# Moving the split weight buffers to other offsets, modulo 512, from the activations in a hybrid decoder layer

## The chip, the cores and the metric

The kernel runs on one core of a Trainium2 chip. TensorE (PE) multiplies, VectorE (DVE) and ScalarE (ACT) work elementwise, GpSimd (POOL) does little here, and SyncE (SP) issues all DMAs. SBUF is the on-chip memory of 128 partitions; an address in it is counted in bytes within a partition. The metric is the device time of one execution in microseconds (us), lower is better. A kernel's time is the median of several runs.

## The reference

One layer on a sequence of 256 tokens of width 2048, in float32: a modulation from a vector c, four token mixers behind one combined input projection, an output projection, a gated FFN with a causal convolution, and a last norm.

```python
mod = (silu(c) @ w_mod + b_mod).reshape(B, 6, D)
sh1, sc1, g1, sh2, sc2, g2 = [mod[:, i, None, :] for i in range(6)]
h = rmsnorm(x, norm_mix) * (1.0 + sc1) + sh1
proj = h @ w_in                                   # 2048 x 5660
y = concat(gla(proj), gated_deltanet(proj), pool(proj), forgetting_attention(proj))
x = x + g1 * (y @ w_out)                          # 2048 x 2048
h = rmsnorm(x, norm_ffn) * (1.0 + sc2) + sh2
gate = causal_dwconv(h @ w_gate, conv_w) + conv_b # 2048 x 5632
x = x + g2 * ((silu(gate) * (h @ w_up)) @ w_down) # 5632 x 2048
return rmsnorm(x, norm_final)
```

## The kernel before

**Three products for one.** Matrices are multiplied in the type fp32r. To keep the accuracy of float32, each operand is split in a high part (the value cast to fp32r) and a low part (what the cast left out), and three products are summed: high by high, high by low, low by high. Activations are split once and kept: `bigA` holds, for each of 16 slices k of the width 2048, the high part of 256 tokens and then the low part; `AH` and `AL` hold the FFN's inner activations. Weights are split as they come. `load` (lines 152 to 156) brings 512 KB into one of five buffers `wr` by a DMA on SP; `load_split` (158 to 163) has ACT cast it into `wh` (line 115) and DVE subtract into `wl` (line 100). There are three buffers `wh` and three `wl`, each 4096 bytes a partition, used in turn.

**The stages and their matmuls**, all recorded on line 97 (`mm`). A matmul has a stationary operand (loaded first, by its own instruction, LDWEIGHTS, 128 columns) and a moving one, which streams.

- Input projection (`gdn`, `pair`): wh or wl stationary, bigA moving, 256 columns; for two of the token-major outputs bigA is stationary and the weights move. Much other work is woven in, above all matrix-vector products of the modulation on DVE (`accumulate`, line 103).
- The mixers, with some input projection between them.
- Output projection (`project`): bigA stationary, wh or wl moving, 512 columns, in the last two chunks 256.
- Gate and up (`proj`): wh or wl stationary, bigA moving. For each k four matmuls of wh with high and low part of bigA side by side, 512 columns, then four of wl with the high part, 256 columns.
- Down projection: AH or AL stationary, wh or wl moving, 512 columns, in the last two chunks 256.

**Where things lie.** Pools take space in SBUF in the order in which they are opened: `keep` first (constants, `bigA`, `bigC`, `ga`, and `x1s` as the last tile), then `wp` (five wr, three wh, three wl, four wm), then the pools of the stages. In the built program bigA starts at 352 modulo 512, and wr, wh, wl, AH and AL all at 416. Every stationary slice (128 columns of 4 bytes) and every step from one k to the next is a multiple of 512 bytes, so the distance of a stationary from a moving operand, modulo 512, is the same for all matmuls of a stage: stationary less moving, called the offset below, is 64 where weights are stationary and bigA moves, 448 where bigA is stationary and weights move, 0 in the down projection.

**What sets the order.** A scheduler orders the instructions of each engine from the program by its own estimate of times, with the waits that follow from the buffers.

Of the kernel before, what the change touches and what calls it, by code (L numbers as in the profile page):

```python
# [8 lines left out]
F32 = mybir.dt.float32  # L9
F32R = mybir.dt.float32r  # L10
# [6 lines left out]
P = 128  # L17
D = 2048
KT = D // P
T = 256  # L20
NT = T // P
# [25 lines left out]
NG = len(GROUPS)  # L47

TAKE = (16, 12, 11)

ORDER = "gpfd"

# [21 lines left out]
def trunk_kernel(ctx: ExitStack, tc: tile.TileContext, x, c, w_mod, b_mod, norm_mix, norm_ffn, w_in,  # L74
# [3 lines left out]
    nc = tc.nc  # L78
# [11 lines left out]
    keep = ctx.enter_context(tc.tile_pool(name="keep", bufs=1))  # L90
    wp = ctx.enter_context(tc.tile_pool(name="wp", bufs=3))

    def kt_(shape, name, dt=F32):
        return keep.tile(shape, dt, name=name, tag=name)
# [19 lines left out]
    def split(hi, lo, src):  # L114
        S_.copy(hi, src)  # L115
        tt(lo, src, hi.bitcast(F32), ALU.subtract)
# [4 lines left out]

    ident = kt_([P, P], "ident")
    nc.sync.dma_start(ident, cst[:, K_ID:K_ID + P])
    crow = kt_([KT, P], "crow")
    nc.sync.dma_start(crow, c[0].rearrange("(k p) -> k p", p=P))
    ones = kt_([P, P], "ones")
    V.memset(ones, 1.0)

# [24 lines left out]
    def load(view, k0, nk, c0, n):  # L153
        wr = wp.tile([P, 1024], F32, name="wr", tag="wr", bufs=5).rearrange("p (k n) -> p k n", n=n)
        nc.sync.dma_start(wr[:, 0:nk], view[:, k0:k0 + nk, c0:c0 + n])  # L155
        return wr

    def load_split(view, k0, nk, c0, n):
        wr = load(view, k0, nk, c0, n)
        wh = wp.tile([P, 1024], F32R, name="wh", tag="wh", bufs=3).rearrange("p (k n) -> p k n", n=n)  # L160
        wl = wp.tile([P, 1024], F32R, name="wl", tag="wl", bufs=3).rearrange("p (k n) -> p k n", n=n)
        split(wh[:, 0:nk], wl[:, 0:nk], wr[:, 0:nk])
        return wh, wl

# [63 lines left out]
    with ExitStack() as ph:  # L228
# [59 lines left out]
        with ExitStack() as st:  # L288
            sp = st.enter_context(tc.tile_pool(name="sp", bufs=1, reuse_waits="tile"))
            acp = st.enter_context(tc.tile_pool(name="acp", bufs=1, space=PSUM, reuse_waits="tile"))  # L290
            xt = sp.tile([P, NT, D], F32, name="xt")
            r1 = sp.tile([P, P], F32, name="r1")
            r2 = sp.tile([54, P], F32, name="r2")
            r3 = sp.tile([2 * NF, P], F32, name="r3")
# [115 lines left out]
            def gdn(g):  # L410
                k0, nk = GROUPS[g]
                for k2 in range(k0, k0 + nk, 2):
                    for c3 in range(3):
                        wh, wl = load_split(wi_v, k2, 2, C_QKV + 512 * c3, 512)
                        for kk in range(2):
                            k = k2 + kk
                            for f in range(4):
                                ft = c3 * 4 + f
                                o = acc[ft // 2][:, ft % 2]
                                fs = slice(f * P, f * P + P)  # L420
                                mm(o, wh[:, kk, fs], HL[:, k, 0:T], start=False, stop=False)
                                mm(o, wh[:, kk, fs], HL[:, k, T:], start=False, stop=False)
                                mm(o, wl[:, kk, fs], HL[:, k, 0:T], start=False, stop=k == KT - 1)
                        yield
# [13 lines left out]
            def pair(p, g0, g1):  # L438
                c0, tok, dst, scale = pairs[p]
                k0, k1 = GROUPS[g0][0], sum(GROUPS[g1 - 1])  # L440
                a = ext().rearrange("p (f t) -> p f t", t=T)
                for ka in range(k0, k1, 4):
                    kb = min(ka + 4, k1)
                    wh, wl = load_split(wi_v, ka, kb - ka, c0, 256)
                    for f in range(2):
                        for k in range(ka, kb):
                            fs = slice(f * P, f * P + P)
                            first, last = f == 0 and k == k0, k == k1 - 1
                            if tok:
                                xh, xl = HL[:, k, fs], HL[:, k, T + f * P:T + f * P + P]  # L450
                                three = ((xh, wh[:, k - ka]), (xh, wl[:, k - ka]), (xl, wh[:, k - ka]))
                            else:
                                xh, xl = HL[:, k, 0:T], HL[:, k, T:]
                                three = ((wh[:, k - ka, fs], xh), (wh[:, k - ka, fs], xl), (wl[:, k - ka, fs], xh))
                            for i, (l, r_) in enumerate(three):
                                mm(a[:, f], l, r_, start=first and i == 0, stop=last and i == 2)
                    yield
                with tc.high_priority():
                    add(dst, a, g0 == 0, scale)
# [10 lines left out]
            def extras(g):  # L470
                ps = range(len(pairs) - TAKE[g], len(pairs)) if g < NG - 1 else range(len(pairs))
                for p in ps:
                    yield from pair(p, done[p], g + 1)
                    done[p] = g + 1
# [472 lines left out]
        chunks = ((0, 512), (512, 512), (1024, 512), (1536, 256), (1792, 256))  # L947
        Y2 = bigA()

        def project(n, a):  # L950
            c0, w = chunks[n]
            nk = 1024 // w
            for j in range(KT // nk):
                ks = order[nk * j:nk * j + nk]
                if n == 0:
                    for k in ks:
                        split(Y2[:, k, 0:T], Y2[:, k, T:], pr[:, k + 4])
                wh, wl = load_split(wo_v, ks[0], nk, c0, w)
                steps = [(kk, k, t) for kk, k in enumerate(ks) for t in range(NT)]
                if n == len(chunks) - 1 and ks[-1] == order[-1]:  # L960

                    steps.sort(key=lambda s: s[2])
                for kk, k, t in steps:
                    st, sp_ = j + kk == 0, nk * j + kk == KT - 1
                    xh, xl = Y2[:, k, t * P:t * P + P], Y2[:, k, T + t * P:T + t * P + P]
                    mm(a[t], xh, wh[:, kk], start=st, stop=False)
                    mm(a[t], xh, wl[:, kk], start=False, stop=False)
                    mm(a[t], xl, wh[:, kk], start=False, stop=sp_)
# [5 lines left out]
        x1 = bigC().rearrange("p (t d) -> p t d", t=NT)  # L974
        for t in range(NT):
            nc.sync.dma_start(x1[:, t], x_v[:, t])
        x1s = kt_([P, NT, len(chunks)], "x1s")
        with tc.tile_pool(name="op", bufs=2, reuse_waits="tile") as op:
            for n, (c0, w) in enumerate(chunks):
                ns, gs = slice(c0, c0 + w), slice(c0 % 1024, c0 % 1024 + w)  # L980
# [11 lines left out]
    with ExitStack() as ph:  # L992
# [51 lines left out]
        with tc.tile_pool(name="gp", bufs=2, reuse_waits="tile") as gp:  # L1044
            for n in range(NF // 4):
                gt = proj(gp, wg_v, 512 * n)
                ut = proj(gp, wu_v, 512 * n)
                for i in range(4):
                    f = 4 * n + i
# [12 lines left out]
        with tc.tile_pool(name="op2", bufs=1, reuse_waits="tile") as op:  # L1062
            chunks = ((0, 512), (512, 512), (1024, 512), (1536, 256), (1792, 256))
            fs = op.tile([P, NT, len(chunks)], F32, name="fs")
            f1 = op.tile([P, 4], F32, name="f1")
            for n, (c0, w) in enumerate(chunks):
# [5 lines left out]
                for g in range(NF // nk):  # L1072
                    wh, wl = load_split(wd_v, nk * g, nk, c0, w)
                    for kk in range(nk):
                        k = nk * g + kk
# [55 lines left out]
```

## Time and profile before

| | us |
|---|---|
| median of 3 runs | 1305.72 |
| lowest and highest | 1299.94, 1308.62 |
| the profiled execution | 1303.01 |
| its span, first to last instruction | 1301.2 |
| busy: PE / DVE / ACT | 1248.5 / 891.0 / 636.7 |

The granted clock of TensorE is 0.985 of full speed over the span; the reductions lie at the start and the end. Busy times of PE are sums of overlapping matmuls merged into stretches. A timeline row gives the start of a run of equal instructions, its length, engine, line, operation, output and inputs, shapes, and how many they are. As matmuls overlap in the pipeline, the length of a row is not their pace; the distance from one row's start to the next one's is.

### The profile page before, as it was taken

The numbers are of one execution on the slowest core, as the hardware profiler recorded it, in microseconds if no ns is written. First come the engines' busy times: TensorE is split into PE (matmuls) and PEld (weight loads), VectorE is DVE, ScalarE is ACT, GpSimd is POOL, SyncE is SP. The second block draws the span as 40 slices with busy tenths as digits, with TensorE's granted clock in tenths as the row PEclk, the third lists the DMA queues.
The fourth block names the chain that finished last, engine by engine and source line by source line (L and its number), as shares of the span: only waits on it lengthen the run. The fifth ranks groups of instructions, "written<-read, shape, count | busy, mean of one in ns | idle before, by whom it ended". The sixth has DMA issues, their size and how long they took to land.

```text
span 1301.2 us, 20372 instructions
## 1 busy us (share of the span) xinstructions
PE 1248.5 (96%) x7927; PEld 1091.0 (84%) x7927; DVE 891.0 (68%) x1201; ACT 636.7 (49%) x1000; POOL 22.7 (2%) x31
## 2 busy tenths in 40 slices
PE   2799999999999999999999999999999999999996
PEld 1799999898876788888888888888888888888896
DVE  7689797989763397676656656665656597964543
ACT  3455344774354454564545555554555454443432
POOL 0200000010000100000000000000000000000000
PEclk9799999999999999999999999999999999999998
DMA  9999998796566988556576666666665699875652
GB/s 321 277 367 378 337 341 290 259 339 212 164 236 240 318 317 276 156 165 192 163 214 190 186 187 193 190 172 206 187 187 163 219 374 359 323 243 194 192 181 81
DMA packets 174231, 311.94 MB, mean 240 GB/s; under 512 B 16172, under 2 KB 65331, under 8 KB 173495
## 3 DMA queue, kind: packets, MB, share of 16 engines
q1 hardware_dynamic: 174135, 310.65, 72.9%
q8 instruction: 62, 1.02, 0.3%
q14 instruction: 34, 0.28, 0.1%
HBM read 308.51 MB, written 2.10 MB: 239 GB/s over the span
## 4 chain that ended last, share of the span: by engine, by line
PE 92%; DMA 4%; SPq 1%; DVE 1%; ACT 1%; issue 1%; POOLq 0%; ACTq 0%; DVEq 0%
PE fpt L97 57%; PE ext L97 16%; PE wot L97 5%; PE gdt L97 4%; PE acc L97 4%; PE bgt L97 3%; DMA wm<-in_w_mod_dram 3%; PE oxt L97 2%; DMA wr<-in_w_in_dram 1%; DVE ga L103 1%; DMA ct<-in_cst_dram 0%; ACT xT L1011 0%; DVE wl L100 0%; SPq L399 0%; SPq L155 0%
## 5 line engine op out<-in xcount | busy, mean ns | idle before, releaser
L100 DVE TENSOR_TENSOR wl<-wr,wh 128x1024 fp32r<-128x1024 f32 x384 | 469.2, 1223 | 293.6 <-ACT wh L115 292.6
L115 ACT CAST wh<-wr 128x1024 fp32r<-128x1024 f32 x384 | 403.4, 1051 | 494.9 <-PE fpt L97 310.8
L97 PE MATMUL fpt<-bigA,wh 128*128 128x512 f32 x1408 | 399.6, 395 | 2.1 <-DVE bigA L103 2.1
L97 PEld LDWEIGHTS fpt<-bigA,wh 128*128 128x128 f32 x1408 | 239.3, 189 | 32.8 <-issue 2.2
L97 PEld LDWEIGHTS fpt<-bigA,wl 128*128 128x128 f32 x1408 | 222.4, 188 | 34.4 <-DVE wl L100 3.6
L97 PE MATMUL fpt<-bigA,wl 128*128 128x256 f32 x1408 | 240.4, 279 | 0.0
L103 DVE SCALAR_TENSOR_TENSOR ga<-wm,cond,ga 128x1024 f32<-128x1024 f32 x139 | 177.8, 1279 | 9.5 <-DMA wm<-in_w_mod_dram 8.6
L97 PE MATMUL fpt<-wl,AH 128*128 128x512 f32 (+1 forms) x440 | 152.9, 348 | 0.0
L97 PE MATMUL fpt<-wh,AL 128*128 128x512 f32 (+1 forms) x440 | 152.5, 347 | 0.0
L97 PE MATMUL fpt<-wh,AH 128*128 128x512 f32 (+1 forms) x440 | 142.5, 348 | 0.0
L97 PE MATMUL ext<-bigA,wh 128*128 128x256 f32 x768 | 137.0, 280 | 0.0
L97 PEld LDWEIGHTS ext<-bigA,wh 128*128 128x128 f32 x768 | 117.3, 188 | 3.1 <-DVE dS L100 0.8
L97 PE MATMUL ext<-bigA,wl 128*128 128x256 f32 x384 | 107.2, 280 | 1.7 <-DVE wl L100 1.7
L97 PEld LDWEIGHTS fpt<-wh,AH 128*128 128x128 f32 x440 | 83.3, 189 | 10.7 <-issue 0.2
L97 PEld LDWEIGHTS fpt<-wh,AL 128*128 128x128 f32 x440 | 83.3, 189 | 10.5 <-issue 0.2
L97 PEld LDWEIGHTS fpt<-wl,AH 128*128 128x128 f32 x440 | 83.3, 189 | 10.5 <-issue 0.2
L97 PE MATMUL acc<-bigA,wh 128*128 128x256 f32 x384 | 70.3, 289 | 4.7 <-ACT bigA L115 2.9
L97 PEld LDWEIGHTS ext<-bigA,wl 128*128 128x128 f32 x384 | 72.1, 188 | 3.0 <-DVE wl L100 2.1
L97 PE MATMUL ext<-wh,bigA 128*128 128x256 f32 (+1 forms) x320 | 68.0, 304 | 0.0
L97 PEld LDWEIGHTS acc<-bigA,wh 128*128 128x128 f32 x384 | 60.7, 198 | 5.1 <-ACT bigA L115 3.0
L97 PE MATMUL wot<-wh,bigA 128*128 128x512 f32 (+1 forms) x256 | 63.2, 337 | 0.0
L97 PEld LDWEIGHTS ext<-wh,bigA 128*128 128x128 f32 x320 | 51.7, 188 | 5.5 <-ACT wh L115 1.7
(340 smaller groups left out, 1191.9 us busy)
## 6 DMA issues: line engine op xcount, KB each, us to landing
wm<-in_w_mod_dram SPq DMA_DIRECT2D x192, 512.0 KB, 5.8
wr<-in_w_in_dram SPq DMA_DIRECT2D x88, 512.0 KB, 9.7
wr<-in_ffn_w_gate_dram SPq DMA_DIRECT2D x88, 512.0 KB, 3.9
wr<-in_ffn_w_up_dram SPq DMA_DIRECT2D x88, 512.0 KB, 4.4
wr<-in_ffn_w_down_dram SPq DMA_DIRECT2D x88, 512.0 KB, 4.5
wr<-in_w_out_dram SPq DMA_DIRECT2D x32, 512.0 KB, 4.2
xt<-in_x_dram SPq DMA_DIRECT2D x2, 1024.0 KB, 7.2
bigC<-in_x_dram SPq DMA_DIRECT2D x2, 1024.0 KB, 8.6
```

The source lines that it names most:

```text
L97: PE.matmul(o, lhsT=l, rhs=r, start=start, stop=stop, skip_group_check=True)
L100: V.tensor_tensor(out=o, in0=a, in1=b, op=op)
L103: V.scalar_tensor_tensor(out=o, in0=a, scalar=s, in1=b, op0=op0, op1=op1)
L115: S_.copy(hi, src)
```

## The change

Three things are done to the layout; no instruction is added or removed.

- Each of the three pairs wh, wl gets a name and a buffer of its own (wh0, wl0, wh1 and so on), used in turn as before, and wl0 and wl1 are padded by 64 and 224 bytes. So the pairs lie at three different places modulo 512.
- x1s, the last tile ahead of the weight buffers, is padded from 64 bytes to 160.
- crow (512 bytes, the row form of c) moves from `keep` to the pool `sp` of the first stage, which makes room.

In the built program bigA stays at 352 modulo 512, wr lies at 0, the pairs at 0, 64 and 288, AH and AL at 288. The offset as defined above is then, for the three pairs, 160, 224 and 448 with stationary weights; 352, 288 and 64 with stationary bigA; 288, 224 and 0 in the down projection.

```diff
+APART = (96, 64, 224)
...
-    crow = kt_([KT, P], "crow")
-    nc.sync.dma_start(crow, c[0].rearrange("(k p) -> k p", p=P))
...
+    loads = [0]
+
     def load_split(view, k0, nk, c0, n):
         wr = load(view, k0, nk, c0, n)
-        wh = wp.tile([P, 1024], F32R, name="wh", tag="wh", bufs=3).rearrange("p (k n) -> p k n", n=n)
-        wl = wp.tile([P, 1024], F32R, name="wl", tag="wl", bufs=3).rearrange("p (k n) -> p k n", n=n)
+        i = loads[0] % 3
+        loads[0] += 1
+        wh = wp.tile([P, 1024], F32R, name=f"wh{i}", tag=f"wh{i}", bufs=1)
+        wl = wp.tile([P, 1024], F32R, name=f"wl{i}", tag=f"wl{i}", bufs=1,
+                     padded_shape=[P, 1024 + (APART + (0,))[i + 1] // 4])
+        wh, wl = (w.rearrange("p (k n) -> p k n", n=n) for w in (wh, wl))
         split(wh[:, 0:nk], wl[:, 0:nk], wr[:, 0:nk])
         return wh, wl
...
             xt = sp.tile([P, NT, D], F32, name="xt")
+            crow = sp.tile([KT, P], F32, name="crow")
+            nc.sync.dma_start(crow, c[0].rearrange("(k p) -> k p", p=P))
...
-        x1s = kt_([P, NT, len(chunks)], "x1s")
+        x1s = keep.tile([P, NT, len(chunks)], F32, name="x1s", tag="x1s", padded_shape=[P, NT, (64 + APART[0]) // 8])
```

The order of the instructions is the same on all engines but for one place, early in the first up pass. On ACT, before (wr_5972 and so on are the loads of w_up, in order; lo copies empty the gate pass):

```order
L115 CAST wh_5974<-wr_5972 128x1024
L115 CAST wh_5996<-wr_5994 128x1024
L115 CAST wh_6018<-wr_6016 128x1024
L1040 COPY lo_5934<-fpt_5754 128x256
L1040 COPY lo_5937<-fpt_5755 128x256
L115 CAST wh_6040<-wr_6038 128x1024
```

and after, where the cast of the fourth load stands ahead of the third's:

```order
L117 CAST wh0_5974<-wr_5972 128x1024
L117 CAST wh2_6018<-wr_6016 128x1024
L117 CAST wh1_5996<-wr_5994 128x1024
L1048 COPY lo_5934<-fpt_5754 128x256
L1048 COPY lo_5937<-fpt_5755 128x256
L117 CAST wh0_6040<-wr_6038 128x1024
```

The same pair on DVE, where the low parts are made, before:

```order
L100 TENSOR_TENSOR wl_5975<-wr_5972,wh_5974 128x1024
L100 TENSOR_TENSOR wl_5997<-wr_5994,wh_5996 128x1024
L100 TENSOR_TENSOR wl_6019<-wr_6016,wh_6018 128x1024
L100 TENSOR_TENSOR fpt_5754<-fpt_5754,lo_5934 128x256
L100 TENSOR_TENSOR fpt_5755<-fpt_5755,lo_5937 128x256
```

and after, in the same exchange of places:

```order
L102 TENSOR_TENSOR wl0_5975<-wr_5972,wh0_5974 128x1024
L102 TENSOR_TENSOR wl2_6019<-wr_6016,wh2_6018 128x1024
L102 TENSOR_TENSOR wl1_5997<-wr_5994,wh1_5996 128x1024
L102 TENSOR_TENSOR fpt_5754<-fpt_5754,lo_5934 128x256
L102 TENSOR_TENSOR fpt_5755<-fpt_5755,lo_5937 128x256
```

TensorE takes the third load before the fourth in both.

## Prediction

> **What bounds the kernel now.** I read the page's busy table and chain of waits first, then the busy time by stage, then the groups of instructions by form, and last the timeline of TensorE, row by row, in each stage.
>
> ```profile
> span 1301.2 us, 20372 instructions
> PE 1248.5 (96%) x7927; PEld 1091.0 (84%) x7927; DVE 891.0 (68%) x1201; ACT 636.7 (49%) x1000; POOL 22.7 (2%) x31
> PE 92%; DMA 4%; SPq 1%; DVE 1%; ACT 1%; issue 1%; POOLq 0%; ACTq 0%; DVEq 0%
> 76.00:265.00 189.00, 186.87 (x1590) 181.81 (x1591) 165.64 (x214) 96.31 (x139) 1.46 (x3) 1.00 0.97 326
> 546.00:1041.00 495.00, 492.43 (x2814) 427.38 (x2815) 313.70 (x457) 264.30 (x405) 0.03 (x1) 1.00 0.62 186
> 1041.00:1190.00 149.00, 149.00 (x653) 122.02 (x652) 115.71 (x114) 64.81 (x78) 0.95 (x1) 1.00 0.85 308
> ```
>
> TensorE is busy 96% of the span and carries 92% of the chain. The three stage rows (stretch, length, then busy time of PE, PEld, DVE, ACT and POOL, then granted clock, DMA share, GB/s) are the input projection, gate and up, and the first part of the down projection: TensorE never idles there for more than 1%, the clock is 1.00, and VectorE, the next engine, has room (166 of 189 us at most, 314 of 495 in gate and up). So nothing that ACT, DVE or the DMAs gain or lose by a few ns shows; what counts is the spacing of the matmuls themselves.
>
> Each matmul is preceded by a load of its stationary operand, and the load of the next one runs while the present one streams. The change moves where in SBUF the one lies relative to the other. So the question is whether the spacing of the matmuls depends on that offset. Durations don't tell (they overlap); starts do.
>
> ```profile
> 740.66 1.09 PE L97 MATMUL fpt<-bigA,wh 128*128 128x512 f32 x4
> 741.59 0.62 PE L97 MATMUL fpt<-bigA,wl 128*128 128x256 f32 x4
> 742.05 1.09 PE L97 MATMUL fpt<-bigA,wh 128*128 128x512 f32 x4
> ...
> 645.14 0.40 PE L97 MATMUL fpt<-bigA,wh 128*128 128x512 f32 x1
> ...
> 646.91 0.40 PE L97 MATMUL fpt<-bigA,wh 128*128 128x512 f32 x1
> ```
>
> Gate and up, offset 64 (stationary wh or wl, less moving bigA, modulo 512). One k is four matmuls of 512 columns, 0.93 us or 232.5 ns each, and four of 256, 0.46 us or 115 ns each: 1.39 us a k, 347 ns for a pair of 512 and 256. For a few k the order of the scheduler alternates the two: five pairs between the last two rows take 1.77 us, 354 ns a pair.
>
> ```profile
> 1189.66 0.62 PE L97 MATMUL fpt<-wh,AH 128*128 128x512 f32 x2
> ...
> 1191.93 0.39 PE L97 MATMUL fpt<-wl,AH 128*128 128x512 f32 x1
> 1249.73 0.28 PE L97 MATMUL fpt<-wh,AL 128*128 128x256 f32 x1
> ...
> 1251.41 0.28 PE L97 MATMUL fpt<-wl,AH 128*128 128x256 f32 x1
> ```
>
> Down projection, offset 0 (stationary AH or AL, less moving wh or wl; in the built program both lie at 416 modulo 512). Ten starts in 2.27 us: 227 ns for 512 columns. Fourteen in 1.68 us: 120 ns for 256. Sum of a pair: 347 ns.
>
> ```profile
> 479.65 0.39 PE L97 MATMUL wot<-wh,bigA 128*128 128x512 f32 x1
> ...
> 482.85 0.39 PE L97 MATMUL wot<-wh,bigA 128*128 128x512 f32 x1
> 533.76 0.28 PE L97 MATMUL wot<-wh,bigA 128*128 128x256 f32 x1
> ...
> 536.00 0.28 PE L97 MATMUL wot<-wl,bigA 128*128 128x256 f32 x1
> 239.72 0.28 PE L97 MATMUL ext<-bigA,wh 128*128 128x256 f32 x1
> 240.90 0.28 PE L97 MATMUL ext<-bigA,wl 128*128 128x256 f32 x1
> 249.75 0.28 PE L97 MATMUL ext<-bigA,wh 128*128 128x256 f32 x1
> 251.00 0.28 PE L97 MATMUL ext<-bigA,wh 128*128 128x256 f32 x1
> ```
>
> Output projection, offset 448 (bigA lies 64 before the weights): fourteen in 3.20 us, 228.6 ns for 512; nineteen in 2.24 us, 117.9 ns for 256; a pair 346.5 ns. Input projection, offset 64, 256 columns: ten starts in 1.18 us between the first two rows (118 ns), eleven in 1.25 us between the last two (114 ns): the same instruction at the same offset settles in one of two paces.
>
> So the spacing does depend on something beside the column count: 227 to 232.5 ns for 512 columns, 114 to 120 for 256, at one clock with no wait. But the pair, 512 and 256, costs 346 to 347 ns at all three offsets: what one size gains the other loses.
>
> **The change, part by part.**
>
> *Order.* Nothing moves on PE, POOL and SP. On ACT and DVE one neighbouring pair of splits changes places, early in the first up pass: the fourth load's split now comes ahead of the third's.
>
> ```profile
> 572.83 1.05 ACT L115 CAST wh<-wr 128x1024 fp32r<-128x1024 f32 x1 [1.68 <-PE fpt L97]
> 575.60 1.05 ACT L115 CAST wh<-wr 128x1024 fp32r<-128x1024 f32 x1 [1.73 <-PE fpt L97]
> 578.63 1.09 PE L97 MATMUL fpt<-bigA,wh 128*128 128x512 f32 x4
> 579.56 0.62 PE L97 MATMUL fpt<-bigA,wl 128*128 128x256 f32 x4
> L100 DVE TENSOR_TENSOR wl<-wr,wh 128x1024 fp32r<-128x1024 f32 x384 | 469.2, 1223 | 293.6 <-ACT wh L115 292.6
> ```
>
> The third load's cast ran at 572.83 and the fourth's, which waits for a buffer that TensorE frees, at 575.60. Changed round, the third's cast ends at about 577.7, ahead of its first use at 578.63. Its low part comes after the fourth's on VectorE: 576.65 and two times 1.22 us give 579.1, against a first use at 579.56. Behind the two on ACT stand the copies that empty the gate pass, about 1 us later; their banks are wanted only by the next gate pass, behind the whole of this up pass. Cost 0; the cover is 0.4 us, and if it were gone the cost would be below 1 us, once.
>
> *crow and x1s.* crow's DMA keeps its place as second on SP, so nothing at the start changes. x1s is only spaced wider for one reduction of ten elements. Both 0.
>
> *ACT and DVE on the moved buffers.* Formerly wr, wh and wl were equal modulo 512; now wr is at 0, the pairs at 0, 64 and 288.
>
> ```profile
> L103 DVE SCALAR_TENSOR_TENSOR ga<-wm,cond,ga x139: 1268/1279/1295, 12.7 to 1146.8; 128x1024 f32<-128x1024 f32 x139
> ```
>
> This operation ran with its two inputs 352 bytes apart early on (wm in the pool sp) and 64 apart later, and lies within 1268 and 1295 ns throughout. So I cost the offset there at 0, under the cover of VectorE's free time.
>
> *TensorE.* New offsets: gate, up and most of the input projection 160, 224 and 448, a third of the loads each; output projection 352, 288 and 64; down projection 288, 224 and 0.
>
> ```profile
> L97 PE MATMUL fpt<-bigA,wh 128*128 128x512 f32 x1408 | 399.6, 395 | 2.1 <-DVE bigA L103 2.1
> L97 PE MATMUL fpt<-wl,AH 128*128 128x512 f32 x264 | 103.1, 391 | 0.0
> L97 PE MATMUL fpt<-wl,AH 128*128 128x256 f32 x176 | 49.8, 283 | 0.0
> L97 PEld LDWEIGHTS fpt<-bigA,wh 128*128 128x128 f32 x1408 | 239.3, 189 | 32.8 <-issue 2.2
> L97 PEld LDWEIGHTS ext<-bigA,wsh 128*28 128x28 f32 x32 | 3.3, 104 | 0.3
> ```
>
> Why should the pair be constant? A load of 128 columns takes 85 ns longer than one of 28: 0.85 ns a column of 4 bytes, some 109 ns for its 512 bytes. The moving operand goes by in 0.44 ns a column (227 / 512), 990 bytes in that time. So in every load the stream overtakes it by nearly 512 bytes, one full turn of the distance that the change sets. If they collide at equal addresses modulo 512, the offset decides when, hardly how often. This is my reading; the three equal pair sums are what bears it out.
>
> Sum. Gate and up: 1408 pairs at 347 ns, change 0. Down projection: 3 x 264 = 792 matmuls of 512 and 3 x 176 = 528 of 256, two thirds of them off the offset 0. Nobody has run 224 or 288; between the ends 227 and 232.5, and 114 and 120, I take the mean of the three offsets that ran, 229.4 for 512 (227, 228.6, 232.5) and 117.6 for 256 (120, 117.9, 115): 528 x 2.4 = +1.3 us and 352 x -2.4 = -0.8 us. Output projection and input projection: as likely to gain as to lose, 0. Together +0.5 us on the profiled execution, 1303.01 (1301.2 of it span): 1303.5 us. The median of the runs shown is 1305.72, so the profiled one stands 0.2% under it.
>
> The ends. All at the best pace seen, 227 and 114: gate and up 1408 x (347 - 341) = -8.4 us, down 528 x -6 = -3.2, input projection up to 4 ns on 1590, -6.4: -18, 1285 us. All at the worst, the alternating 354 ns for a pair: 1408 x 7 = +9.9, down 792 x 5.5 = +4.4, input projection +6: +20, 1323 us.
>
> A rule that speaks against the change: the Trainium skill, TensorE: Matmul & The Clock Gate, part 2, says that PE has two independent SBUF read ports, and that loading the next weights takes no read bandwidth from the running matmul. By that rule offsets would cost nothing anywhere and the sum would be 0, 1303 us. The rows agree only in part: they show a matmul of 512 columns at 227 in one place and at 232.5 ns in another with nothing waited for.
>
> **Rivals.**
>
> *Far offsets collide less (faster).* All offsets seen are 0 or 64 either way; 160, 224, 288 and 352 lie far from them. If collisions need nearness, two of the three pairs drop to the best pace, and perhaps the third. For it: 114 ns held for 1.25 us at one offset. Against it: three offsets with one pair sum. Price: up to the whole -18, 1286 us when most of it comes. It decides when a k of gate and up falls under 1.37 us for two of three buffers.
>
> *A worse phase (slower).* The new distances set the long matmuls to collide in every load, as in the alternating order: a pair at 354 ns and the down projection's 512 at 232.5. Price +14 to +20, 1319 us. For it: the matmul of 512 takes 5.5 ns more at 64 than at 0, so losing a good offset in the down projection is real. Against it: the alternating pace came with another order. It decides when a k takes 1.41 us or more.
>
> *It does nothing at all.* The paces are of order, not of address; then every row stays and the time is 1303 us. Its outcome is in the first case.
>
> **How the numbers follow.** Unchanged within 1% (either that the pair sum holds, or that gains and losses by buffer cancel): 0.61. Far offsets: 0.26. Worse phase: 0.13. One per cent, 13 us, is about what a measurement of this kernel can tell from no change; 1286 and 1319 lie just beyond it on each side. The time is that of the likeliest, 1303.5 us; its own range is 1293 to 1314. The range for 8 in 10 takes in both rivals up to their prices: 1285 to 1319.
>
> **What would show it.** In the profile after, gate and up: rows of four wh and four wl alternating with one k in 1.37 to 1.40 us, perhaps with three values that repeat every third load. Down: 512 columns at 227 to 232 ns, 256 at 114 to 120. A k under 1.36 us at any buffer, or 512 columns under 226 ns, would refute the constant pair; a k of 1.41 would be the slower rival. A wait of TensorE for wl near 579 us would be the swapped splits.

## The result, and the profile after

The changed kernel takes 1311.91 us (median of 8 runs, 1310.17 to 1315.08), the one before 1303.95 (8 runs, 1299.94 to 1308.62): ratio 1.0066, 95% interval 1.0050 to 1.0081. So it is slower by more than its measurement is uncertain and by less than 1%. The profiled execution took 1315.08, the slowest of the eight, and the one of before 1303.01, 0.9 under its median; of the 12.1 us between the two traces some 4 are scatter of single runs.

The page of the changed kernel: span, busy times, and the shares of the chain.

```profile
span 1313.3 us, 20372 instructions
PE 1261.4 (96%) x7927; PEld 1098.5 (84%) x7927; DVE 890.8 (68%) x1201; ACT 635.4 (48%) x1000; POOL 23.5 (2%) x31
PE 93%; DMA 3%; DVE 1%; SPq 1%; ACT 1%; issue 1%; POOLq 0%; ACTq 0%; DVEq 0%
```

PE is busy 12.9 us longer with the same 7927 matmuls; DVE and ACT are where they were. Busy time by stage, the three stretches that the prediction showed, and the two groups that split the weights:

```profile
76.00:265.00 189.00, 186.50 (x1560) 181.30 (x1559) 162.51 (x211) 94.36 (x134) 1.45 (x3) 1.00 0.92 316
546.00:1041.00 495.00, 492.34 (x2813) 427.85 (x2812) 313.73 (x462) 264.68 (x411) 0.70 (x1) 1.00 0.63 185
1041.00:1190.00 149.00, 149.00 (x653) 120.00 (x652) 114.79 (x113) 63.35 (x76) 0.95 (x1) 1.00 0.83 304
```

```profile
L102 DVE TENSOR_TENSOR wl<-wr,wh 128x1024 fp32r<-128x1024 f32 x384 | 469.1, 1223 | 300.2 <-ACT wh L117 299.7
L117 ACT CAST wh<-wr 128x1024 fp32r<-128x1024 f32 x384 | 402.4, 1048 | 498.3 <-PE fpt L99 317.9 <-PE ext L99 61.9 <-PE wot L99 33.5
```

The clock is 1.00 and TensorE as full as before in each stretch, and 189 us of input projection hold 1560 matmuls where they held 1590. The split of a load costs what it did (1223 and 1048 ns). TensorE waits no longer than before; the matmuls themselves stand further apart. Gate and up, timeline of TensorE, the first row of each k over four loads (the rows of wl between them left out):

```profile
859.69 1.09 PE L99 MATMUL fpt<-bigA,wh 128*128 128x512 f32 x4
...
861.10 1.10 PE L99 MATMUL fpt<-bigA,wh 128*128 128x512 f32 x4
...
862.51 1.09 PE L99 MATMUL fpt<-bigA,wh 128*128 128x512 f32 x4
...
863.91 1.10 PE L99 MATMUL fpt<-bigA,wh 128*128 128x512 f32 x4
...
865.31 1.08 PE L99 MATMUL fpt<-bigA,wh 128*128 128x512 f32 x4
...
866.68 1.07 PE L99 MATMUL fpt<-bigA,wh 128*128 128x512 f32 x4
...
868.07 1.09 PE L99 MATMUL fpt<-bigA,wh 128*128 128x512 f32 x4
...
869.48 1.10 PE L99 MATMUL fpt<-bigA,wh 128*128 128x512 f32 x4
```

From start to start 1.41, 1.41 | 1.40, 1.40 | 1.37, 1.39 | 1.41: a load is two k, and three values follow each other, one for each pair of buffers, where before every k took 1.39. Down projection, 512 columns, then 256:

```profile
1191.13 0.40 PE L99 MATMUL fpt<-wl,AH 128*128 128x512 f32 x1
...
1195.80 0.40 PE L99 MATMUL fpt<-wl,AH 128*128 128x512 f32 x1
...
1197.19 0.39 PE L99 MATMUL fpt<-wl,AH 128*128 128x512 f32 x1
...
1198.78 0.39 PE L99 MATMUL fpt<-wh,AL 128*128 128x512 f32 x1
...
1255.73 0.28 PE L99 MATMUL fpt<-wh,AH 128*128 128x256 f32 x1
...
1258.13 0.28 PE L99 MATMUL fpt<-wh,AL 128*128 128x256 f32 x1
1258.24 0.28 PE L99 MATMUL fpt<-wh,AH 128*128 128x256 f32 x1
...
1260.61 0.28 PE L99 MATMUL fpt<-wh,AL 128*128 128x256 f32 x1
```

Twenty steps in 4.67 us between the first two rows are 233.5 ns, over two loads; then seven in 1.59, 227 ns, in the third. With 256 columns twenty steps take 2.40 us (120 ns), and twenty behind them 2.37 (118.5).

For the whole trace, the mean distance from one matmul's start to the next one's, in ns, by stage, columns and the offset that the built program's addresses give (a step counts with the matmul that starts it; steps that hold a wait, over 25 ns longer than the stream, are left out; "in" is the input projection with weights stationary, and "out" the output projection from its second chunk on):

```
                 before            after, by offset
gate/up  512     64: 232.2         160: 233.5   224: 232.9   448: 229.8
gate/up  256     64: 115.1         160: 119.2   224: 117.1   448: 116.6
in       256     64: 115.3         160: 119.9   224: 116.8   448: 117.7
out      512    448: 229.0         352: 234.0   288: 233.4    64: 233.4
out      256    448: 117.8         352: 117.3   288: 118.3    64: 114.7
down     512      0: 226.8         288: 233.6   224: 233.3     0: 228.9
down     256      0: 120.0         288: 118.4   224: 116.8     0: 119.3
```

Times the counts this is +3.3 us in gate and up (1408 pairs: the 256 columns +2.5 ns, the 512 -0.2), +4.7 in the input projection (2.7 ns x 1728), +0.7 in the output projection (its first chunk, 96 more matmuls of 512 columns, adds +0.4), and +4.1 - 0.9 in the down projection (792 x 5.1, 528 x -1.8), together about +12, the distance of the two traces. The medians are only 8.0 us apart; by the table of parts below, gate and up, the output and the down projection make 7.2 of them, so the input projection's share is the uncertain one.

### The profile page after: what moved, and what is told of

Same layout as the page of the kernel before. It is cut to its first block, busy times and chain, and to the rows that moved or that the text cites. A ratio compares the mean times of both kernels' runs of the same rounds, so it can differ in the third digit from the quotient of the medians.

```text
span 1313.3 us, 20372 instructions
## 1 busy us (share of the span) xinstructions
PE 1261.4 (96%) x7927; PEld 1098.5 (84%) x7927; DVE 890.8 (68%) x1201; ACT 635.4 (48%) x1000; POOL 23.5 (2%) x31
## 4 chain that ended last, share of the span: by engine, by line
PE 93%; DMA 3%; DVE 1%; SPq 1%; ACT 1%; issue 1%; POOLq 0%; ACTq 0%; DVEq 0%
PE fpt L99 57%; PE ext L99 16%; PE wot L99 5%; PE acc L99 4%; PE gdt L99 4%; PE bgt L99 3%; DMA wm<-in_w_mod_dram 3%; PE oxt L99 2%; DVE ga L105 1%; DMA wr<-in_w_in_dram 0%; ACT xT L1019 0%; ACT wh L117 0%; SPq L407 0%; DVE wl L102 0%; PE oxt L881 0%
## 5 line engine op out<-in xcount | busy, mean ns | idle before, releaser
L102 DVE TENSOR_TENSOR wl<-wr,wh 128x1024 fp32r<-128x1024 f32 x384 | 469.1, 1223 | 300.2 <-ACT wh L117 299.7
L117 ACT CAST wh<-wr 128x1024 fp32r<-128x1024 f32 x384 | 402.4, 1048 | 498.3 <-PE fpt L99 317.9
L99 PE MATMUL fpt<-bigA,wl 128*128 128x256 f32 x1408 | 243.9, 281 | 0.0
L99 PE MATMUL ext<-bigA,wh 128*128 128x256 f32 x768 | 140.1, 282 | 0.0
```

The source lines that it names most:

```text
L99: PE.matmul(o, lhsT=l, rhs=r, start=start, stop=stop, skip_group_check=True)
L102: V.tensor_tensor(out=o, in0=a, in1=b, op=op)
```

## Experiments

Two theories stood at the start. *Values*: each offset has a pace of its own, and the three that the kernel before happened to use are low ones. *Mixture*: the pace suffers from buffers at different offsets following each other, whatever the offsets. *Bookkeeping* (names, the moved crow, the exchanged splits) was to be excluded first.

The length of each part in all profiled kernels, from the start of TensorE's first matmul there to the next part's first, us (the first column begins with the span and takes in the output projection's first chunk; the last ends with its last matmul's start):

```
                      to out   out     gate/up   down
before                473.93   75.32   492.69    246.31
after                 478.74   75.96   496.18    249.42
e1  all at 64         474.74   75.32   492.42    246.31
e2  all at 224        476.76   76.22   496.03    246.30
e3  all at 320        473.19   75.33   492.72    246.34
e4  192 / 240 / 240   473.33   75.11   490.16    246.13
e5  gate/up at 28     476.02   75.34   506.86    246.34
e6  gate/up at 32     476.69   75.33   497.84    246.31
e7  28 / 120 / 120    475.70   75.23   507.00    245.91
e8  28, by weights    476.60   75.35   490.32    248.26
```

Where addresses did not change, the last three columns repeat within 0.3 us (out and down within 0.05). The first, which holds work woven in from other engines, scatters by some 3 us: in e1, e3, e5, e6 and e7 the input projection's offset is that of before modulo 256, and the part takes 473.2 to 476.7 us.

**e1: all pairs at 64 again.** The change's names, crow's move and the exchanged splits stay.

```diff
-APART = (96, 64, 224)
+APART = (0, 0, 0)
```

> The changed kernel with all three pairs of weight buffers back at 64 bytes beyond the activations; their own names, the moved crow and the exchanged pair of splits stay. Values (each offset has a pace of its own): as before the change, ratio 1.000 within 0.002, gate and up 512 columns at 232.2 ns and 256 at 115.1, down 226.8 and 120.0. Mixture (the loss comes of a different offset at every load): the same, 1.000. Bookkeeping (crow, names, the exchange of splits cost it): ratio about 1.006.

Measured 1303.49 us, ratio 1.0003 (0.9989 to 1.0017); gate and up 232.3 + 115.0 ns, down 226.8 and 120.0. The loss is in the addresses, and none that can be measured in the bookkeeping.

**e2: all pairs at 224.** The down projection goes back to 0.

```diff
-APART = (96, 64, 224)
+APART = (160, 0, 0)
```

> All three pairs at 224 bytes beyond the activations, one uniform offset; the down projection is back at offset 0. Values: gate and up keep what the second pair showed in the changed kernel, 232.9 ns for 512 columns and 118.0 for 256, so 351 for a pair against 347.3: 1408 x 3.6 = +5 us; input projection 116.8 against 115.3, +2.4 us; output projection at offset 288, +2 us; together +9 us, ratio 1.007, though the down projection is back at 226.8 and 120.0. Mixture: uniform loads fall back into step, gate and up 347 ns a pair, ratio 1.000 within 0.002.

Measured 1309.94 us, ratio 1.0044 (1.0029 to 1.0058). Matmuls of gate and up in the 400 us from 600 to 1000 us of the span, in the kernel before, the changed one and this one, in that order:

```profile
600.00:1000.00 400.00, 400.00 (x2294) 1.00 0.63 189
```

```profile
600.00:1000.00 400.00, 400.00 (x2277) 1.00 0.64 188
```

```profile
600.00:1000.00 400.00, 400.00 (x2279) 1.00 0.63 187
```

With nothing mixed, gate and up still lose: 232.4 + 117.1 ns, +3.3 us by the table of parts; the down projection, back at 0, loses nothing. So mixture is not the cause. The ratio is below the 1.007 that values expected: gate and up lost 3.3 us in place of 5 and the output projection 0.9 in place of 2, while the input projection's pace, 116.8 ns, is the expected one. For gate and up the expectation took 118.0 ns for 256 columns. One comes near that (117.9) when the steps that lead into the next buffer are counted with the next one; counted where they start it is the 117.1 of the table, which is what this run shows.

**m1 and m2: the paces by themselves.** Matmuls of this type alone, no layer: at each of 32 offsets, 16 bytes apart, 64 of 512 columns, 64 of 256, and 8 times 4 and 4 as in gate and up; in m2 both operands lie 32 bytes further.

```python
st = lambda i: S[:, e + 128 * (i % 16):e + 128 * (i % 16) + 128]   # e = offset / 4
for i in range(64): mm(a, st(i), M[:, i // 4 % 8])                 # 512
for i in range(64): mm(a[:, 0:256], st(i), M[:, i // 4 % 8, 0:256])
for k in range(8):                                                 # 4 + 4
    for f in range(4): mm(a, st(4 * k + f), M[:, k])
    for f in range(4): mm(a[:, 0:256], st(4 * k + f + 8), M[:, k, 0:256])
```

> Leaves the whole layer out: only matmuls in fp32r on two SBUF tiles, at 32 offsets of the stationary from the moving operand, 0 to 496 bytes in steps of 16; at each 64 matmuls of 512 columns, 64 of 256, and 8 times 4 of 512 and 4 of 256. The moving operand starts at 0 modulo 64. Values: pace of 512 columns about 227 ns near offset 0 and about 233 at 160 to 352; of 256 columns about 120 at 0, 113 to 115 at 64, 117 to 119 far off. If neither engine traffic nor history but the offset alone sets the pace, each offset has one pace. Mixture: all offsets alike, within 1 ns, as each is held for 64 matmuls. If the excess over 2.4 GHz came of the moving operand's misalignment to 64 bytes, 512 columns here take 213 to 216 ns.

> The same sweep with both tiles 32 bytes further, so that the moving operand starts at 32 modulo 64, as bigA does in the kernel. Values: the same curve against the offset as the aligned sweep, within 1 ns. If alignment to 64 bytes matters: another curve, at least 5 ns per 512 columns apart.

The means of m1 in ns (offsets 256 to 496 repeat those of 0 to 240 within 0.3):

```
offset    0     16    32    48    64    80    96    112   128   144   160   176   192   208   224   240
512     226.9 233.3 233.4 233.3 233.3 232.0 234.3 233.3 232.4 233.3 233.3 230.0 228.9 231.9 233.3 226.7
256     120.0 118.3 118.3 118.3 113.3 118.8 117.3 120.0 118.7 118.4 120.1 118.1 117.8 116.7 116.7 117.3
4+4     350.8 351.4 350.7 350.1 346.7 350.1 352.4 350.6 350.9 353.3 353.1 348.4 345.8 348.4 350.0 348.3
```

m2 has the same curve but for a few values (512 columns 226.7 at 16 and 233.3 at 208, 256 columns 117.8 at 64 and 120.0 at 144), and its floor is no lower. The means leave out the first 8 steps of the two long patterns and the first 16 of the third, in which the pace settles. Nothing but TensorE works here, as m1's page says:

```profile
PE 1117.7 (98%) x6208; PEld 954.6 (84%) x6208; DVE 3.5 (0%) x1; ACT 7.6 (1%) x6; POOL 0.2 (0%) x4
```

So the traffic of ACT, DVE and the DMAs is not what sets the paces. And they are the kernel's own: down before at 0, 226.8 and 120.0; out at 448, which is 192 here, 229.0 and 117.8. In gate and up the agreement is closer than the means above show. Of the 352 k, 291 have the sweep's order, four of 512 and four of 256; in the others the sizes alternate or passes meet, and the means mix the two kinds. In the 291 (a dozen of them, which hold a wait, left out), a pair takes 346.7 ns in the kernel before (m1 at 64: 346.7), and in the changed kernel 352.7, 349.8 and 345.8 for its three buffers (m1 at 160, 224 and 192: 353.1, 350.0 and 345.8); in e2 it takes 350.0. The lowest two of the sixteen pairs are at 64 and 192 (mean of all 350.1), and 0 has nearly the lowest value for 512 columns. The kernel before sat on the low points; no run tells of a reason for it, and the equal pair sums that the prediction built on are a coincidence of three of them.

**e3: all pairs at 320.**

```diff
-APART = (96, 64, 224)
+APART = (256, 0, 0)
```

> All three pairs at an offset of 320 from bigA, 256 bytes beyond the 64 of the kernel before; everything else is as in the changed kernel. Period theory (the pace is set by stationary less moving address modulo 256, as the sweep of offsets read): every row as before the change, gate and up 232 and 115 ns, down 227 and 120 ns, time as before, ratio 1.000. Rival (the address modulo 512 decides, as the 'far offsets' and 'phase' rivals of the prediction had it, and the sweep's equal halves are a property of its short loops): gate and up at another pace, 117 to 120 ns for the 256 columns as at the changed kernel's offsets, ratio 1.004 to 1.008.

Measured 1302.82 us, ratio 0.9996 (0.9982 to 1.0009). Timeline of gate and up:

```profile
739.96 1.09 PE L99 MATMUL fpt<-bigA,wh 128*128 128x512 f32 x4
...
741.35 1.09 PE L99 MATMUL fpt<-bigA,wh 128*128 128x512 f32 x4
...
742.73 1.09 PE L99 MATMUL fpt<-bigA,wh 128*128 128x512 f32 x4
```

A k of 1.39 us, as before; 232.2 + 115.1 (346.7 a pair in the 291 k), down 226.8 and 120.0. The period of 256 bytes holds in the kernel.

**e4: a low point for each stage.** Weights at 64 from bigA (modulo 256), the activations' views moved inside larger buffers: gate and up 192, output and down projection 240.

```diff
-    bigA = lambda: keep.tile([P, KT, 2 * T], F32R, name="bigA", tag="bigA")
+    def bigA(e=0):
+        w = keep.tile([P, KT * 2 * T + 32], F32R, name="bigA", tag="bigA")
+        return w[:, e:e + KT * 2 * T].rearrange("p (k n) -> p k n", n=2 * T)
...
-        Y2 = bigA()
+        Y2 = bigA(12)
...
-        H2 = bigA()
+        H2 = bigA(32)
```

> Each stage at an offset that the sweep showed as cheap: in-projection at 64 as before, gate and up at 192, the output projection at 240, down at 240 (all modulo 256; the weights stay together, the views of the activations are moved inside their buffers). Values theory (each offset has its own pace, and the sweep's carry over to the kernel): gate and up 228.9 + 117.8 in place of 232.2 + 115.1 a pair, -0.9 ns x 1408 to -2.1 us; down 256 columns 117.3 in place of 120, -1.4 us; output projection 226.7 in place of 229, -0.6 us; in all -3 to -4.3 us, ratio 0.9967 to 0.9975. Rival (paces depend on the entry and the mix so much that the sweep doesn't carry over): 1.000 or above.

Measured 1302.40 us, ratio 0.9998 (0.9985 to 1.0011): not the gain that was expected. Gate and up went to 230.5 + 116.1 ns (346.6 over all, 346.0 in the 291 k, where m1 had 345.8) and its part is 2.5 us shorter; the 256 columns of the down projection fell to 117.3, but its 512 rose to 228.4, where m1 had 226.7, and the output projection's 512 took 228.4. The three parts together are 2.9 us shorter in the profiled execution, and the medians show nothing of it; the scatter of the first part, some 3 us, is as large.

**m3: fewer columns in each load.** m1's first two patterns with stationary operands of 32, 64 and 128 columns.

> Matmuls alone, the whole layer is left out. 16 offsets in steps of 16 bytes, stationary operands of 32, 64 and 128 columns, 64 matmuls of 512 and 64 of 256 columns each. Collision theory (the stationary load's reads and the stream's reads collide in banks by the address modulo 256, and each collision holds up the stream): with a quarter of the columns loaded the pace above the floor of 226.7 and 113.3 shrinks to about a quarter, so 512 columns at most 228.5 instead of 233.4 ns. Rival (the offset sets when a load may start or is handed over, one fixed price for each matmul): the curve keeps its height, 6 to 7 ns, whatever the number of columns loaded.

```
columns loaded     512, mean (low to high)     256, mean (low to high)
 32                231.1 (226.7 to 240.0)      115.6 (113.3 to 117.9)
 64                231.0 (226.7 to 235.6)      117.2 (113.3 to 120.0)
128                231.9 (226.7 to 234.3)      118.0 (113.3 to 120.0)
```

The slowest of all, offset 32 with 32 columns, and the same with 128; behind the colon the shortest, middle and longest matmul in ns, then the first and the last start:

```profile
L48 PE MATMUL longquarterc<-M,S x64: 387/399/422, 71.4 to 86.5; 128*32 128x512 f32 x64
...
L48 PE MATMUL longfullc<-M,S x64: 395/396/500, 800.5 to 815.3; 128*128 128x512 f32 x64
```

A quarter of the load takes 15.1 us for 63 steps, 240 ns each, the whole load 14.8. For 512 columns the curve keeps its height, though not its shape (at 224 it is 226.7 ns with 32 columns and 233.3 with 128), so the price is not a sum of collisions in proportion to what is loaded; for 256 columns it falls by half with 32 columns, so this is only partly told apart.

**m4: steps of 4 bytes.** m2's three patterns at 64 offsets.

> Matmuls alone, the whole layer is left out. Offsets 0 to 252 in steps of 4 bytes; 64 matmuls of 512, 64 of 256, and 4 + 4 as in gate and up at each. Smooth-curve theory: neighbours within a ns of each other between the points of the sweep by 16, with the pair of gate and up at 345 to 354 ns, the lowest near 192 and 240. Rival (several stable paces at each offset, and which one is taken depends on how the pattern is entered): neighbours 4 bytes apart jump by 3 to 6 ns with no trend, and points at multiples of 16 don't repeat the earlier sweep.

The pair runs from 343.3 (offset 28) to 356.8 (204), mean 350.5; 512 columns from 226.7 to 237.3, 256 from 113.3 to 120.8. Neighbours jump: 349.1, 343.3, 350.3 at 24, 28, 32; 348.5, 356.8, 350.0 at 200, 204, 208. At multiples of 16 m2's pair values repeat within half a ns, all but 144 (350.0 against 353.4). There is no smooth curve. Single gaps show why: at 0 they settle into 227, 227, 226 and so on, at 8 into 234, 230, 231, 229, 230, five by five. At these offsets the steps fall into a rhythm that closes on itself.

**e5, e6 and e7: the fine sweep's low point in the kernel.** Gate and up at 28, the same at 32, and 28 together with 120 in the output and down projections; weights as in e1, views moved as in e4.

```diff
-        H2 = bigA()
+        H2 = bigA(9)
```

(e6: 8; e7: 9, with Y2 moved by 46 and AH and AL by 30 elements of 4 bytes.)

> All weights' parts back at one place (offset 64 modulo 256 in the input projection, 192 in the output projection, 0 in the down projection, as before the change), but the view of bigA that gate and up read is moved by 36 bytes inside its buffer, so that gate and up alone have an offset of 28. Values theory: the fine sweep's value at 28 carries over, 226.8 + 116.4 ns a pair in place of 347.3, -4 ns x 1408 = -5.7 us, ratio 0.9957. Rival (the rhythm that a stage falls into depends on how it is entered, so the best point of a sweep means nothing elsewhere): a pair at 346 to 350 ns, ratio 0.999 to 1.003.

> The same with an offset of 32, four bytes further. Values theory: 231.6 + 118.7 ns a pair, +3.0 ns x 1408 = +4.2 us, ratio 1.0032, 9.9 us above the kernel with 28. Rival (entry decides, or neighbours are alike): equal to the kernel with 28.

> Gate and up at 28, output and down projection at 120, the input projection at 64 (all modulo 256). Values theory: gate and up -5.7 us; down 226.7 and 116.7 ns in place of 226.8 and 120.0, -3.3 ns x 528 = -1.7 us; output projection 226.7 and 116.7 in place of 229.0 and 117.8, -0.6 us; together -8.0 us, ratio 0.9939. Rival (entry decides): above 0.997.

Measured: e5 1319.12 us, ratio 1.0118 (1.0099 to 1.0137); e6 1309.47, 1.0049 (1.0033 to 1.0064); e7 1317.42, 1.0109 (1.0086 to 1.0131). Timeline of gate and up in e5:

```profile
861.49 1.11 PE L99 MATMUL fpt<-bigA,wh 128*128 128x512 f32 x4
862.44 0.65 PE L99 MATMUL fpt<-bigA,wl 128*128 128x256 f32 x4
...
865.79 1.11 PE L99 MATMUL fpt<-bigA,wh 128*128 128x512 f32 x4
```

and in e6:

```profile
860.91 1.09 PE L99 MATMUL fpt<-bigA,wh 128*128 128x512 f32 x4
861.84 0.64 PE L99 MATMUL fpt<-bigA,wl 128*128 128x256 f32 x4
...
865.13 1.09 PE L99 MATMUL fpt<-bigA,wh 128*128 128x512 f32 x4
```

Three k take 4.30 us in e5 (236.8 + 120.8 ns, 357.6 a pair) and 4.22 in e6 (231.8 + 119.2, 351.0); in the 291 k it is 358.3 and 350.8. So 32 came as the sweep had it (350.3), and 28, in e5 and e7 alike, as the worst pace seen in any kernel, where the sweep had its best. By the parts, e5's gate and up is 14.2 us longer, with out and down unchanged. One thing differed from the sweep: there the stationary operand had been moved, here the moving one, to an address 4 bytes past a multiple of 32.

**m5: the same offset entered in four ways**, behind five matmuls of 512, 384, 320 or 288 columns.

> Matmuls alone, the whole layer is left out. Eight offsets (0, 16, 28, 32, 64, 120, 192, 240), each pattern (64 of 512, 64 of 256, 8 times 4 + 4) entered four times behind five matmuls of 512, 384, 320 or 288 columns. Values theory: the four entries of an offset settle within 1 ns of each other, whatever came ahead. Entry theory: at some offsets two paces or more, 3 to 6 ns apart, as 113.3 and 117.8 ns at an offset of 64 in the two sweeps by 16.

Most values settle within 0.3 ns, but some don't: 512 columns 233.3 three times and 226.7 once at 16, 226.7 or 228.3 at 240; 256 columns 116.7 or 119.4 at 120, 117.8 three times and 113.3 once at 192; the 512 of the 4 + 4 pattern 226.9 three times and 233.5 once at 28. Offset 16, the first and the fourth entry, first and last start of 64:

```profile
L48 PE MATMUL longbp<-M,S x64: 392/396/509, 179.6 to 194.4; 128*128 128x512 f32 x64
...
L48 PE MATMUL longbs<-M,S x64: 388/389/499, 294.5 to 308.9; 128*128 128x512 f32 x64
```

14.8 against 14.4 us for the same instructions at the same addresses. So an offset can have two paces, and what came ahead picks one; behind the same neighbours it stays the same (m2: 226.7 at 16 and at 272). e4's 228.4 in the down projection (240) and e7's 119.4 there (120) agree with such second paces. 357 is not among them.

**e8: 28 with the moving operand in place.** In gate and up the weights' views are moved by 220 bytes, bigA stays; wh and wl are slices of one tile.

```diff
-    def load_split(view, k0, nk, c0, n):
+    W = wp.tile([P, 6 * 1024 + 64], F32R, name="W", bufs=1)
+    def load_split(view, k0, nk, c0, n, e=0):
...
+        wh, wl = (W[:, e + 1024 * j:e + 1024 * j + 1024].rearrange("p (k n) -> p k n", n=n) for j in (2 * i, 2 * i + 1))
...
-                wh, wl = load_split(view, 2 * g, 2, c0, 512)
+                wh, wl = load_split(view, 2 * g, 2, c0, 512, 55)
```

> Gate and up at an offset of 28 once more, but with bigA left where it was (32 modulo 64) and the weights' views moved by 220 bytes in this stage alone; wh and wl are slices of one tile for that, which lets some casts and, in the down projection, some matmuls stand in another order. Alignment theory (the pace goes by the offset only while the moving operand lies at a multiple of 32 bytes; with 28 it lay at 4 modulo 64 in the run before): gate and up at the fine sweep's 226.8 + 116.4 = 343 ns a pair, -5.7 us, ratio 0.995 to 0.997. Entry theory (the sweep's 28 has two rhythms, one of them at 233.5 + 116.6, and a kernel falls into any): 350 ns, ratio 1.003. If the offset of 28 as such were bad in the kernel: 357 ns again, ratio 1.011.

Measured 1305.18 us, ratio 1.0010 (0.9994 to 1.0026): the whole shows no gain, the stage does. Its pace is 228.1 + 117.0 ns, 345.0 a pair. In the 291 k both of m5's rhythms at 28 come up in the kernel: 245 k take 343.3 ns a pair and 31 take 350.0. Busy time in gate and up and behind it:

```profile
546.00:1041.00 495.00, 491.68 (x2844) 431.76 (x2844) 314.85 (x462) 266.89 (x415) 0.69 (x1) 1.00 0.63 187
1041.00:1190.00 149.00, 146.82 (x636) 119.22 (x637) 114.49 (x113) 63.88 (x76) 0.95 (x1) 1.00 0.85 306
```

2844 matmuls in the stretch that held 2814 before; from the first to the last start of the stage it is 4.7 us shorter. But at its end TensorE stands still for 2.2 us, which before it didn't, and waits for a cast on ACT:

```profile
PE fpt L99 <- ACT W L117: 2.2, 1, 2.2
```

The down projection is 1.9 us longer; the one tile gives it another order, and what each of the two costs was not taken apart. At 28 as such there is nothing bad, so the place of the moving operand is left as the cause in e5.

**m6: both operands moved together.** The offset stays, the moving operand's own place changes.

```python
st = lambda i: S[:, (off + d) // 4 + 128 * (i % 16):(off + d) // 4 + 128 * (i % 16) + 128]
mv = lambda k, n=512: M[:, d // 4 + 512 * (k % 8):d // 4 + 512 * (k % 8) + n]
```

> Matmuls alone, the whole layer is left out. Offsets 28, 32, 64, 120 and 192, each with both operands moved together by 0, 4, 8, 12, 16, 20, 28, 32, 36 and 48 bytes, so that the offset stays and only the moving operand's own place changes. Alignment theory: at 0, 16, 32 and 48 the values of the fine sweep, at 4, 36 and the other odd places slower, at offset 28 moved by 4 some 357 ns for the 4 + 4 pattern as in the kernel with the shifted view. Entry theory: no trend with the place, values within the two or three paces that the offset showed before.

A pair of the 4 + 4 pattern, ns, by offset (row) and the place of the moving operand (column; M itself lies at a multiple of 64):

```
          0      4      8      12     16     20     28     32     36     48
 28     343.3  358.2  355.0  348.3  351.8  356.6  352.6  343.3  358.2  351.8
 32     350.7  357.2  353.4  346.8  353.2  356.7  346.6  350.2  357.2  353.2
 64     346.7  359.0  355.8  349.3  345.2  358.4  353.3  346.7  359.0  345.2
120     346.6  353.3  355.0  345.1  350.1  358.3  348.3  346.6  353.3  350.1
192     345.9  356.7  353.4  345.0  345.1  356.5  344.0  345.8  356.6  345.2
```

Offset 28 with the moving operand at 0, at 4 and at 32, first and last start of the 64 matmuls:

```profile
L47 PE MATMUL mixap<-M,S x64: 277/337/497, 50.0 to 61.0; 128*128 128x512 f32 x32, 128*128 128x256 f32 x32
...
L47 PE MATMUL mixaq<-M,S x64: 280/340/502, 84.8 to 96.2; 128*128 128x512 f32 x32, 128*128 128x256 f32 x32
...
L47 PE MATMUL mixaw<-M,S x64: 277/337/497, 294.0 to 305.0; 128*128 128x512 f32 x32, 128*128 128x256 f32 x32
```

11.0, 11.4 and 11.0 us. The place counts modulo 32: 32, 36 and 48 repeat 0, 4 and 16, and 4 and 20 cost 353 to 359 at every offset. e5's 358.3 is this table's 358.2. The stationary operand moves along in this run, but it is not its place that counts: in e5 it lay at a multiple of 32, in e8 at 28 beyond one. In the change itself all moving operands lie at multiples of 32, so there the offset decided, and what a buffer's matmuls ran behind.

No version ran faster than the kernel before by more than a measurement tells: e3 and e4 are equal to it, and most of e8's 4.7 us in its stage is paid back at the stage's end and in the down projection.

## Why the prediction was off

The forecast was no change, 1303.5 us; it became 1311.91, inside the range (1285 to 1319) and within 1%, but slower by more than the interval. That one per cent is what a measurement can tell was too cautious: eight runs of each kernel tell 0.50 to 0.81% from no change. By its steps:

- *What bounds the kernel.* Right. Where addresses change, a stage grows by its spacing, and e5's out and down, whose addresses stay, are as before.
- *Order, exchanged splits: 0.* Right. In the changed kernel the third load's cast is the last ahead of the copies; ACT, DVE and TensorE in the timeline:

```profile
581.16 1.05 ACT L117 CAST wh<-wr 128x1024 fp32r<-128x1024 f32 x1 [1.74 <-PE fpt L99]
582.24 1.22 DVE L102 TENSOR_TENSOR wl<-wr,wh 128x1024 fp32r<-128x1024 f32 x1 [1.56 <-ACT wh L117]
584.25 1.09 PE L99 MATMUL fpt<-bigA,wh 128*128 128x512 f32 x4
585.18 0.63 PE L99 MATMUL fpt<-bigA,wl 128*128 128x256 f32 x4
585.64 1.10 PE L99 MATMUL fpt<-bigA,wh 128*128 128x512 f32 x4
```

The low part ends at 583.46 and TensorE's rows follow each other without a wait at 585.18; the cover is 1.7 us, more than the 0.4 that was worked out. The fourth load's cast did not wait as long as was thought: it ran a load earlier, at 578.37, and the two only exchanged their turns.

- *crow, x1s, ACT and DVE on the moved buffers: 0.* Right: e1 at 1.0003, and 1223 and 1048 ns as before.
- *"The pair, 512 and 256, costs 346 to 347 ns at all three offsets", and so gate and up 0 and input projection 0.* This is the step that failed. Three offsets were taken for all. The sweeps have the pair between 343 and 357, mean 350, and the three that the kernel before used are among its lowest; at the new ones a pair of gate and up takes 352.7, 349.8 and 345.8 in place of 346.7. The reason given, that in every load the stream overtakes it once round the distance and the offset only moves the moment, is not borne out: the price does depend on the offset, with a period of 256 bytes and not 512 (e3), and for 512 columns a quarter of the load costs as much as the whole (m3). Gate and up lost 3.3 us, the input projection up to 4.7, of which some 3 can't be told from the scatter of its part.
- *Down projection +1.3 - 0.8.* Right in sign for both sizes, and mis-sized for the 512 columns: 792 x 5.1 = +4.1 us in place of +1.3. The mean of three known offsets was a poor guess for two unknown ones (233.3 and 233.6), and the load at 0 took 228.9 in place of 226.8. In m4 the first gaps at 0 are 240, 235, 233, 236, 224, 231, 236, 228, 233, 231, and only then 227 and 226, and a load here holds but 12 matmuls. The changed kernel's trace shows the same at each change of buffer: over its 22 loads at 0 the first five steps take 230, 236, 229, 233 and 230 ns (medians) and the other seven 227, which makes the 228.9; in the rows above, six steps from 1195.80 are 232 ns and the seven from 1197.19 are 227. So a mixture of buffers did cost something here, 264 x 2.1 ns or 0.6 us. 256 columns: -0.9.
- *Output projection 0.* +0.7 us and +0.4 in its first chunk, its 512 columns from 229.0 to 233.6.
- *Rival "far offsets collide less".* Refuted: 160 and 224 are slower than 64. Only 448 gained, 0.9 ns a pair in the 291 k.
- *Rival "a worse phase".* It came in part. The down projection's 512 went to 233.5, past the 232.5 that it named; gate and up's pair to 352.7 and 349.8 for two buffers, not 354 for all. So the price was 8 us in place of 14 to 20. Its sign of a k at 1.41 us showed for one pair of buffers in three.
- *Rival "it does nothing; the paces are of order".* Refuted by e1 and e2, which have one order and differ.
- *The Trainium skill*, TensorE: Matmul & The Clock Gate, part 2, says that PE has two independent SBUF read ports and that loading the next weights takes no read bandwidth from the running matmul. As the prediction read it, no offset would then cost anything. The measurement decides otherwise: 512 columns settle anywhere from 226.7 to 240 ns in the sweeps, by address, at a granted clock of 0.998 or more and with no other engine at work. That a load of 32 columns costs 512 columns as much as one of 128 would agree with a load that takes no bandwidth; what the two share, no run here shows.

## What to carry to other kernels

The few values that a kernel shows are no sample of those that it doesn't: three offsets with one pair sum looked like a law, and were three of the lowest. Before a layout is moved, run the bare inner loop at the new addresses; here that sweep told the kernel's pace to within 1 ns a pair wherever the order was the sweep's, the moving operand lay as in the sweep, and the same one of two rhythms was entered. Compare with the steps of that order, and not with a stage's mean, which mixes orders. Where weights are loaded for every matmul, watch two addresses, stationary less moving modulo 256 and the moving operand modulo 32; here they were worth 0.4 to 1.2% of the time (e2, e5).

## What the runs showed of the hardware that was not expected

- The pace of such matmuls repeats with 256 bytes of the distance between stationary and moving operand (e3; m1 within 0.3 ns), and with 32 bytes of the moving operand's place (m6). No settled pace of a sweep lay below 226.7 ns for 512 columns and 113.3 for 256.
- A difference of 4 bytes is worth up to 7 ns a pair in the distance (28 against 32, m4) and up to 15 in the moving operand's place (28 at 0 and at 4, m6).
- The same instructions at the same addresses can settle in two rhythms, 226.7 or 233.3 ns at 16, 113.3 or 117.8 at 192, by what ran ahead of them (m5); in e8 one stage holds both of its offset's, 343.3 and 350.0 a pair. A new rhythm takes some steps to settle, five of a load's twelve in the changed down projection. Why there are rhythms, and what load and stream share, stays open.
